# First layer of a fused four-layer kernel: the compression network of the keys loaded early, and compressed attention moved ahead of the local pairs

## The chip, the cores and the metric

The kernel runs on one core of one Trainium2 chip. The metric is device time in microseconds (us) of one execution; where several executions were timed, the median is given. One further execution was taken by the hardware profiler, and the rows below are of that one.

## The reference, cut to what matters

256 tokens of 1024 numbers go through two layers of attention and feed-forward, and then through two mixer blocks. All of it is float32. The change touches the attention of the first layer alone. That layer has eight "A" heads with three gated branches and eight "B" heads with a sliding window and sinks:

```python
def compress_blocks(t, pe, w1, w2):
    chunks = t.reshape(bsz, hkv, seq // CMP_STRIDE, CMP_STRIDE, dh)
    blocks = jnp.concatenate([chunks[:, :, :-1], chunks[:, :, 1:]], axis=-2)
    blocks = (blocks + pe).reshape(bsz, hkv, nc, CMP_BLOCK * dh)
    return jax.nn.silu(blocks @ w1) @ w2          # w1: 2048 x 256
...
# layer 0
z = h @ w_in_e                                    # queries, six key/value groups, gates, B's q, k, v
kc, vc = compress_blocks(akc, pe_k, wk1, wk2), compress_blocks(avc, pe_v, wv1, wv2)
o_cmp = softmax(q_plain . kc) . vc                # 15 compressed tokens
o_sel = softmax(q_rot . selected keys) . values
o_win = softmax(q_rot . window keys) . values
a_out = g0 * o_cmp + g1 * o_sel + g2 * o_win
x = x + concat(a_out, swa_sink_attention(bq, bk, bv, sinks)) @ w_out_e
```

With 256 tokens the selected branch sees every causal block, so both o_sel and o_win are plain causal attention with different keys.

## The kernel before

The tokens lie as two tiles of 128 partitions. A dense product of this kernel is three TensorE passes (`mm3`, lines 249 to 252): activations and weights are each split into a high and a low part of the type fp32r, and high times high, high times low and low times high are added up in one PSUM bank. The weights come from memory in the order of the program: SP issues one DMA after another (`load`, line 175; `raw_block`, line 216) into five buffers of 128x1024 float32 that are named `wr`. A block is split by ScalarE, which writes the high part `wh` (line 236), and by VectorE, which subtracts it and writes the low part `wl` (line 237). `wh` and `wl` have five buffers each. A DMA into a `wr` buffer waits until the last reader of the block before has ended.

The order of the instructions of each engine is fixed when the program is built: a scheduler takes the program as it is written, with its own estimate of durations, and fills each engine's queue. PSUM has two banks for `psd` tiles, four for `psb` and two for `psm`; one attention pair takes two of the four `psb` banks.

The first layer's input projection w_in_e comes in chunks. Chunk 0 (selected keys and values, raw keys for compression, gates) and chunk 1 (the A queries, with and without rotation, `qr` and `qp`) stand first. `chunk2()` makes the window keys and values, the raw values for compression and the B keys. `chunk3()` and `chunk4()` make the B values and the B queries, in four blocks of 128x768 and two of 128x1024; `bq` (line 688) rotates a query tile, transposes it (line 693) and copies it out on ScalarE.

Around these stand the attention steps. `attend` (line 349) does two heads: products of queries and keys (line 358, a stretch of 64 rows for each head, so that two heads can stand side by side in the array), mask and maximum on VectorE (line 366), exponential on ScalarE (line 367), six transposes on TensorE (line 375), a copy of the transposed probabilities on VectorE for one head (line 381) and ScalarE for the other (line 379), and the products with the values (line 358 again). `nsa_pair(br, j)` calls it for branch br (0 selected, 1 window) and heads 2j and 2j+1 and adds into `accA` (lines 398 and 727); `b_pair(j)` does so for the B heads into `accB`.

`compress` (line 636) builds the blocks (line 640 on TensorE, 647 and 649 on VectorE), multiplies them with the 2048 x 256 weights (line 656, 64 products of 32 columns by 256, unsplit float32 straight from `wr`), transposes and sums, and applies SiLU. `keys_cmp` and `values_cmp` use it; each loads its weights as four blocks of 128x1024 into `wr`, and a block stays there until the products of line 656 are done. `attend_cmp` is the attention on the 15 compressed tokens: scores (line 774), a chain of ten VectorE steps with one exponential on ScalarE (lines 781 to 792), transposes (795), a ScalarE copy (797), the products with the compressed values (800) and the addition into `accA` (801). At the end `split_T` (line 265) transposes `accA` and `accB` (line 270), and the output projection w_out_e follows.

Of the kernel before, what the change touches and what calls it, by code (L numbers as in the profile page):

```python
# [18 lines left out]
P = 128  # L19
# [4 lines left out]
BLK = 1024  # L24
# [123 lines left out]
def model(ctx: ExitStack, tc: tile.TileContext, A, out, taps=None):  # L148
    nc = tc.nc
# [66 lines left out]
    def raw_block(src, off, n):  # L216
        raw = tmp([BLK], "wr", "wr")
        load(raw[:, :n], bass.AP(tensor=src.tensor, offset=src.offset + off, ap=[[n, P], [1, n]]))
        return raw
# [332 lines left out]
    def layer0(nm, after):  # L552
# [69 lines left out]
        kz = {0: keys_T(ksd)}  # L622

        w = win.get(1)
        for t in range(2):
            o = psb()
            dense(o, nm.T(t), w)
            r = nm.rstd[t]
            q0 = tmp([512], "w512", "q0")
            nc.scalar.activation(q0, o, AF.Copy, scale=r)  # L630
            q1 = tmp([512], "w512", "q1")
            rope(q1.rearrange("p (h d) -> p h d", h=8), o.rearrange("p (h d) -> p h d", h=8), r, 8, 64, t)
            headsT(qr, q1, t)
            headsT(qp, q0, t)

        def compress(dup, pe_b, w1):
            p = psm()
            for g in range(2):
                for t in range(2):
                    nc.tensor.transpose(p[:, g * 256 + t * P:g * 256 + (t + 1) * P],  # L640
                                        dup[t][:, g].rearrange("p a d -> p (a d)"), ident)
            b = tmp([2, 256], "w512", "blk")
            pg = p.rearrange("p (g t) -> p g t", g=2)
            ij = lambda x: x.rearrange("p g (i j) -> p g i j", j=16)
            for a in range(2):
                s = slice(64 * a, 64 * a + 64)
                nc.vector.tensor_tensor(ij(b[s, :, 0:240]), ij(pg[s, :, 16 * a:16 * a + 240]),
                                        pe_b[s, None, None, :].to_broadcast([64, 2, 15, 16]), op=ALU.add)
            nc.vector.tensor_copy(b[:, :, 240:256], pg[:, :, 240:256])
            bj = b.rearrange("p g (i j) -> p (g i) j", j=16)  # L650
            ph = psm()

            for part in range(4):
                wt = raw_block(w1, part * P * BLK, BLK)
                for j in range(4):
                    nc.tensor.matmul(ph[32 * j:32 * j + 32, :256], bj[:, :, part * 4 + j], wt[:, j * 256:(j + 1) * 256],
                                     start=(part == 0), stop=(part == 3), skip_group_check=True)
            z = tmp([256], "qk", "cz")
            nc.scalar.activation(z, ph[:, :256], AF.Copy)
            p2 = psm()  # L660
            for cb in range(2):
                nc.tensor.transpose(p2[:, cb * P:(cb + 1) * P], z[:, cb * P:(cb + 1) * P], ident)
            e, h, u = (small(64, n_) for n_ in ("ce", "ch", "cu"))
            nc.vector.tensor_reduce(u.rearrange("p (a b) -> p a b", a=2), p2[:, :256].rearrange("p (a c b) -> p a b c", a=2, c=4),
                                    axis=AX.X, op=ALU.add)
            nc.scalar.activation(e, u, AF.Exp, scale=-1.0)
            nc.vector.tensor_scalar(e, e, 1.0, None, op0=ALU.add)
            nc.vector.reciprocal(e, e)
            nc.vector.tensor_tensor(h, u, e, op=ALU.mult)
            return h  # L670
# [25 lines left out]
        def chunk3():  # L696

            w = win.get(3)
            for t in range(2):
                o = psd()  # L700
                dense(o[:, :384], nm.T(t), w)
                nc.scalar.activation(vt[t][:, 2, :, 0:64], hv2(o[:, 0:128]), AF.Copy, scale=nm.rstd[t])
                bq(o[:, 128:384], qb[0], nm.rstd[t], t)
# [38 lines left out]
            weighted(pair_of(accB, j), pov, rc)  # L742

        def keys_cmp():
            hk = compress(kcd, pe[:, 0, :], A["cmp_k_w1"])
            pk = psm()
            for cb in range(2):
                nc.tensor.matmul(pk[:, :32], w2k[:, cb].rearrange("p a d -> p (a d)"), hk[:, cb * 32:(cb + 1) * 32],
                                 start=(cb == 0), stop=(cb == 1))
            for g in range(2):  # L750
                nc.vector.tensor_copy(kcz[g][0:64, 0, 0:15], pk[0:64, g * 16:g * 16 + 15])
                nc.vector.tensor_copy(kcz[g][64:128, 1, 0:15], pk[64:128, g * 16:g * 16 + 15])

        def values_cmp():
            hv = compress(vcd, pe[:, 1, :], A["cmp_v_w1"])
            hvx = tmp([2, 8, 16], "qk", "hvx")
            for cb in range(2):
                for g in range(2):
# [48 lines left out]
            return lambda k: (mixT[t, k // 4][0][:, k % 4, :], mixT[t, k // 4][1][:, k % 4, :])  # L807

        nsa_pair(0, 0)
        nsa_pair(0, 1)  # L810
        chunk2()
        nsa_pair(0, 2)
        keys_cmp()
        nsa_pair(0, 3)
        nsa_pair(1, 0)
        nsa_pair(1, 1)
        nsa_pair(1, 2)
        vbd = values_cmp()
        nsa_pair(1, 3)
        chunk3()  # L820
        chunk4()
        attend_cmp(vbd)
        b_pair(0)
        b_pair(1)
        b_pair(2)
# [529 lines left out]
```

## Time and profile before

| what | value |
|---|---|
| three runs | 1586.75, 1581.74, 1588.69 us; median 1586.75 us |
| profiled execution | 1581.74 us, of which the span (first to last instruction) is 1580.0 us |
| TensorE busy | 1557.5 us, 99% of the span |
| VectorE, ScalarE, GpSimd busy | 982.3, 855.3, 140.3 us |
| data moved by DMA | 269.53 MB, mean 171 GB/s |
| granted TensorE clock | 0.9 or more of full speed in all 40 slices |

The profile gives each engine's busy time, the instructions with their durations, the granted clock, and for each idle stretch what ended it. PE is TensorE, DVE is VectorE, ACT is ScalarE, POOL is GpSimd, and SPq is the queue on which SP issues the weight DMAs. The stretch that the change touches runs from about 20 us, where chunk 1 is being multiplied, to about 127 us, where the output projection of the first layer is being multiplied.

### The profile page before, as it was taken

Reading aid. Unit: us, or ns where it says so; the run is one execution under the profiler, and the core shown is the slowest. Engines: PE = TensorE matmul, PEld = TensorE weight load, DVE = VectorE, ACT = ScalarE, POOL = GpSimd, SP = SyncE. Lnnn points to the kernel's source line nnn. Section 1 sums busy time; section 2 is a strip of 40 time slices with the busy share of each in tenths; the row PEclk is TensorE's granted clock in tenths of the full one; section 3 lists DMA queues with packets and bytes.
Section 4 is the critical chain, followed back from the end, with each engine's and each line's share of the span. In section 5 each row is a group of like instructions: output and inputs, shape, how many; then the busy total and the mean of one; then the engine's idle time right before and its main releaser. Section 6 shows DMA issues by size and latency. Waiting matters only on the chain.

```text
span 1580.0 us, 21686 instructions
## 1 busy us (share of the span) xinstructions
PE 1557.5 (99%) x7870; PEld 1314.7 (83%) x7870; DVE 982.3 (62%) x1778; ACT 855.3 (54%) x1385; POOL 140.3 (9%) x226
## 2 busy tenths in 40 slices
PE   8999999999999999999999999999999999999997
PEld 7778888899888888899888888888898888888886
DVE  6685545577765455576677655456575777655556
ACT  6555444455454444676474654446685564644445
POOL 2000000011100000120033000000020023000001
PEclk9999999999999999999999999999999999999999
DMA  7424655544545565451657555554552656465661
GB/s 270 149 92 133 206 184 184 187 141 131 182 131 191 186 192 188 161 180 40 196 179 233 174 181 192 186 188 160 177 169 71 204 189 197 161 201 185 197 195 61
DMA packets 80587, 269.53 MB, mean 171 GB/s; under 512 B 11360, under 2 KB 12768, under 8 KB 80480
## 3 DMA queue, kind: packets, MB, share of 16 engines
q1 hardware_dynamic: 80048, 267.10, 52.7%
q8 instruction: 62, 1.02, 0.3%
q10 hardware_dynamic: 432, 1.05, 0.2%
q14 instruction: 45, 0.37, 0.1%
HBM read 267.06 MB, written 1.05 MB: 170 GB/s over the span
## 4 chain that ended last, share of the span: by engine, by line
PE 96%; DVE 2%; ACT 1%; DMA 1%; issue 0%; POOL 0%; POOLq 0%; SPq 0%; DVEq 0%; ACTq 0%
PE psb L250 13%; PE psb L252 13%; PE psb L251 13%; PE psd L252 12%; PE psd L250 12%; PE psd L251 12%; PE psb L358 5%; PE psm L250 3%; PE psm L251 3%; PE psm L252 3%; PE psb L375 1%; PE psb L497 1%; DVE wl L237 1%; PE psb L270 1%; PE psm L270 1%; DMA wr<-w_in_e 1%
## 5 line engine op out<-in xcount | busy, mean ns | idle before, releaser
L237 DVE TENSOR_TENSOR wl<-wr,wh 128x1024 fp32r<-128x1024 f32 (+2 forms) x504 | 598.1, 1198 | 423.0 <-ACT wh L236 410.5
L236 ACT ACTIVATE wh<-wr 128x1024 fp32r<-128x1024 f32 (+2 forms) x504 | 512.6, 1029 | 474.0 <-PE psb L252 208.5
L251 PE MATMUL psb<-wl,th 128*128 128x512 f32 x912 | 349.4, 391 | 0.0
L252 PE MATMUL psb<-wh,tl 128*128 128x512 f32 x912 | 349.2, 390 | 0.0
L250 PE MATMUL psb<-wh,th 128*128 128x512 f32 x912 | 346.5, 391 | 0.0
L252 PE MATMUL psd<-wh,tl 128*128 128x512 f32 (+4 forms) x696 | 255.7, 370 | 3.4 <-DVE tl L279 3.4
L250 PE MATMUL psd<-wh,th 128*128 128x512 f32 (+4 forms) x696 | 258.2, 375 | 0.0
L251 PE MATMUL psd<-wl,th 128*128 128x512 f32 (+4 forms) x696 | 255.0, 369 | 0.5 <-DVE wl L237 0.5
L252 PEld LDWEIGHTS psb<-wh,tl 128*128 128x128 f32 x912 | 171.2, 188 | 35.7
L250 PEld LDWEIGHTS psb<-wh,th 128*128 128x128 f32 x912 | 171.3, 188 | 35.3
L251 PEld LDWEIGHTS psb<-wl,th 128*128 128x128 f32 x912 | 171.3, 188 | 35.2
L252 PEld LDWEIGHTS psd<-wh,tl 128*128 128x128 f32 x696 | 131.2, 188 | 22.7 <-DVE tl L279 5.0
L251 PEld LDWEIGHTS psd<-wl,th 128*128 128x128 f32 x696 | 131.5, 189 | 17.5 <-DVE wl L237 0.9
L250 PEld LDWEIGHTS psd<-wh,th 128*128 128x128 f32 x696 | 131.3, 189 | 17.5 <-issue 1.7
L306 POOL TENSOR_SCALAR rest<-ss 128x1 f32<-128x1 f32 x24 | 7.2, 299 | 919.4 <-ACT junk L316 919.4
L367 ACT ACTIVATE pr<-pr,m 128x128 f32<-128x128 f32 (+1 forms) x144 | 58.3, 447 | 29.9 <-DVE m L366 28.1
L250 PE MATMUL psd<-wh,hth 128*128 128x512 f32 x176 | 71.9, 412 | 0.0
L251 PE MATMUL psd<-wl,hth 128*128 128x512 f32 x176 | 68.8, 391 | 0.0
L251 PE MATMUL psm<-wl,hth 128*128 128x512 f32 x176 | 68.5, 389 | 0.0
L250 PE MATMUL psm<-wh,hth 128*128 128x512 f32 x176 | 68.5, 389 | 0.0
L252 PE MATMUL psm<-wh,htl 128*128 128x512 f32 x176 | 67.8, 389 | 0.0
L487 ACT ACTIVATE sg<-psb,r 128x256 f32<-128x256 f32 x88 | 41.8, 475 | 48.0 <-PE psb L252 47.8
(320 smaller groups left out, 1759.9 us busy)
## 6 DMA issues: line engine op xcount, KB each, us to landing
wr<-w_gate_up SPq DMA_DIRECT2D x176, 512.0 KB, 4.3
wr<-w_down SPq DMA_DIRECT2D x88, 512.0 KB, 3.3
wr<-w_in SPq DMA_DIRECT2D x88, 512.0 KB, 4.0
wr<-w_qkv_o SPq DMA_DIRECT2D x32, 384.0 KB, 3.5
wr<-w_o SPq DMA_DIRECT2D x16, 512.0 KB, 4.1
wr<-w_ple_gate SPq DMA_DIRECT2D x16, 512.0 KB, 4.0
wr<-w_in_e SPq DMA_DIRECT2D x10, 512.0 KB, 4.7
wr<-w_out_e SPq DMA_DIRECT2D x8, 512.0 KB, 4.6
```

The source lines that it names most:

```text
L236: nc.scalar.activation(hi[:, :m * n], raw, AF.Copy)
L237: nc.vector.tensor_tensor(lo[:, :m * n], raw, hi[:, :m * n].bitcast(F32), op=ALU.subtract)
L250: first = nc.tensor.matmul(o, xh, wh, start=start, stop=False)
L251: nc.tensor.matmul(o, xh, wl, start=False, stop=False)
L252: nc.tensor.matmul(o, xl, wh, start=False, stop=stop)
L270: turns.append(nc.tensor.transpose(p[:, j * P:(j + 1) * P], src[:, j * P:(j + 1) * P], ident))
L306: nc.gpsimd.tensor_scalar(rest, ms, self.eps, None, op0=ALU.add)
L358: mm = lambda o, l, r, a, b: nc.tensor.matmul(o, l, r, start=a, stop=b, skip_group_check=True)
L367: exps.append(nc.scalar.activation(e, e, AF.Exp, bias=neg, scale=-1.0))
L375: nc.tensor.transpose(bank[j][:, b * P:(b + 1) * P], pr[:, j, b * P:(b + 1) * P], ident)
L487: nc.scalar.activation(sg, o[:, :256], AF.Silu, scale=r)
L497: nc.tensor.transpose(pt[:, j * 256 + t * P:j * 256 + (t + 1) * P], hs[t][:, j * P:(j + 1) * P], ident)
```

## The change

The change loads the keys' compression weights ahead of chunk 2's weights, as eight DMAs of 128x512 into buffers named `xt` (there are 16 of them; the layer's norm uses eight, the transposed mixed heads use eight later) instead of four DMAs of 128x1024 into `wr`. The order of the calls becomes: pair (0,0), `keys_cmp`, pair (0,1), chunk 2, `values_cmp`, pairs (0,2) and (0,3), `attend_cmp`, pairs (1,0), (1,1) and (1,2), chunk 3, pair (1,3), chunk 4, the four B pairs, the output projection. Line numbers behind `chunk1` move by 6 to 10: what was 656 is 662, 693 is 699, 727 is 733, 781 to 792 are 791 to 802, 795 is 805, 797 is 807, 800 is 810 and 801 is 811. The product of `values_cmp` with its second weights, line 764, is line 774 after the change, and the scores of compressed attention, line 774, are line 784.

```diff
@@ -622,6 +622,12 @@
         kz = {0: keys_T(ksd)}
 
         w = win.get(1)
+
+        w1k = []
+        for h in range(8):
+            w1k.append(tmp([512], "xt", "w1"))
+            at = A["cmp_k_w1"].offset + (h // 2) * P * BLK + (h % 2) * 512
+            load(w1k[h], bass.AP(tensor=A["cmp_k_w1"].tensor, offset=at, ap=[[BLK, P], [1, 512]]))
         for t in range(2):
             o = psb()
             dense(o, nm.T(t), w)
@@ -651,9 +657,9 @@
             ph = psm()
 
             for part in range(4):
-                wt = raw_block(w1, part * P * BLK, BLK)
+                wt = w1(part)
                 for j in range(4):
-                    nc.tensor.matmul(ph[32 * j:32 * j + 32, :256], bj[:, :, part * 4 + j], wt[:, j * 256:(j + 1) * 256],
+                    nc.tensor.matmul(ph[32 * j:32 * j + 32, :256], bj[:, :, part * 4 + j], wt[j],
                                      start=(part == 0), stop=(part == 3), skip_group_check=True)
             z = tmp([256], "qk", "cz")
             nc.scalar.activation(z, ph[:, :256], AF.Copy)
@@ -742,7 +748,7 @@
             weighted(pair_of(accB, j), pov, rc)
 
         def keys_cmp():
-            hk = compress(kcd, pe[:, 0, :], A["cmp_k_w1"])
+            hk = compress(kcd, pe[:, 0, :], lambda part: [w1k[2 * part + j // 2][:, j % 2 * 256:j % 2 * 256 + 256] for j in range(4)])
             pk = psm()
             for cb in range(2):
                 nc.tensor.matmul(pk[:, :32], w2k[:, cb].rearrange("p a d -> p (a d)"), hk[:, cb * 32:(cb + 1) * 32],
@@ -752,7 +758,11 @@
                 nc.vector.tensor_copy(kcz[g][64:128, 1, 0:15], pk[64:128, g * 16:g * 16 + 15])
 
         def values_cmp():
-            hv = compress(vcd, pe[:, 1, :], A["cmp_v_w1"])
+            def w1(part):
+                wt = raw_block(A["cmp_v_w1"], part * P * BLK, BLK)
+                return [wt[:, j * 256:(j + 1) * 256] for j in range(4)]
+
+            hv = compress(vcd, pe[:, 1, :], w1)
             hvx = tmp([2, 8, 16], "qk", "hvx")
             for cb in range(2):
                 for g in range(2):
@@ -807,19 +817,19 @@
             return lambda k: (mixT[t, k // 4][0][:, k % 4, :], mixT[t, k // 4][1][:, k % 4, :])
 
         nsa_pair(0, 0)
+        keys_cmp()
         nsa_pair(0, 1)
         chunk2()
+        vbd = values_cmp()
         nsa_pair(0, 2)
-        keys_cmp()
         nsa_pair(0, 3)
+        attend_cmp(vbd)
         nsa_pair(1, 0)
         nsa_pair(1, 1)
         nsa_pair(1, 2)
-        vbd = values_cmp()
+        chunk3()
         nsa_pair(1, 3)
-        chunk3()
         chunk4()
-        attend_cmp(vbd)
         b_pair(0)
         b_pair(1)
         b_pair(2)
```

Three places of the new order matter below. The first is SP's queue, the weight DMAs of the first layer, before (`wr<-w_in_e 128x1024 x8` is chunks 1 and 2, `128x768` chunk 3, the next two chunk 4):

```order
L176 DMA w2v<-cmp_v_w 128x128
L176 DMA wr<-w_in_e 128x1024 x8
L176 DMA wr<-cmp_k_w 128x1024 x4
L176 DMA wr<-cmp_v_w 128x1024 x4
L176 DMA wr<-w_in_e 128x768 x4
L176 DMA wr<-w_in_e 128x1024 x2
L176 DMA wr<-w_out_e 128x1024 x8
```

and after:

```order
L176 DMA w2v<-cmp_v_w 128x128
L176 DMA wr<-w_in_e 128x1024 x4
L176 DMA w_325<-cmp_k_w 128x512
...
L176 DMA w_339<-cmp_k_w 128x512
L176 DMA wr<-w_in_e 128x1024 x4
L176 DMA wr<-cmp_v_w 128x1024 x4
L176 DMA wr<-w_in_e 128x768 x4
L176 DMA wr<-w_in_e 128x1024 x2
L176 DMA wr<-w_out_e 128x1024 x8
```

The keys' weights moved from behind chunk 2 to ahead of it and out of the `wr` buffers; the values' weights stay ahead of chunks 3 and 4 and hold four of the five `wr` buffers until their products are done.

The second place is TensorE's queue at compressed attention. Before, with `hvx` the hidden compressed values, `qp` the unrotated queries, `cs` the scores, `ppT` their transposed probabilities and `vbd` the compressed values:

```order
L774 MATMUL psm<-kcz_194,qp 128x32 x2
L774 MATMUL psm<-kcz_196,qp 128x32 x2
L358 MATMUL psb<-vt,pt 128x65 x6
...
L375 MATMUL psb<-S,pr 128x128 x9
L358 MATMUL psb<-vt,pt 128x65 x6
L375 MATMUL psb<-S,pr 128x128 x3
L358 MATMUL psb<-vt,pt 128x65 x3
L795 MATMUL psm<-S,cs 128x128 x2
...
L800 MATMUL psm<-vbd,ppT 128x512 x2
```

and after:

```order
L358 MATMUL psb<-vt,pt 128x65 x6
L774 MATMUL psm<-w2v,hvx 128x64
L784 MATMUL psm<-kcz_194,qp 128x32 x2
L784 MATMUL psm<-kcz_196,qp 128x32 x2
L784 MATMUL psm<-kcz_194,qp 128x32 x2
L784 MATMUL psm<-kcz_196,qp 128x32 x2
L774 MATMUL psm<-w2v,hvx 128x64
L805 MATMUL psm<-S,cs 128x128 x2
L810 MATMUL psm<-vbd,ppT 128x512 x2
L699 MATMUL psm<-S,q_1030 128x128 x2
L699 MATMUL psm<-S,q_1067 128x128 x2
L358 MATMUL psb<-kz,qr 128x128
```

Before, two B pairs' products stand between the scores and the transposes of the probabilities; after, one product of 64 columns. All dense products of chunks 3 and 4 stand ahead of this piece after the change.

The third place is ScalarE's queue where the splits of the first w_out_e blocks stand. Before (`pr` is the exponential of a pair, `cz` the compression network's first layer):

```order
L236 ACTIVATE wh_1084<-wr_1082 128x1024
L367 ACTIVATE pr_802<-pr_802,m_801 128x256
L666 ACTIVATE ce_920<-cu_922 128x64
L236 ACTIVATE wh_1400<-wr_1398 128x1024
L702 ACTIVATE vt_190<-psd_1002,r_171 128x2x64
L379 ACTIVATE pt_803<-psb_805 128x384
L236 ACTIVATE wh_1406<-wr_1404 128x1024
```

and after:

```order
L236 ACTIVATE wh_1408<-wr_1406 128x1024
L665 ACTIVATE cz_727<-psm_702 128x256
L236 ACTIVATE wh_1414<-wr_1412 128x1024
L236 ACTIVATE wh_1446<-wr_1444 128x1024
L367 ACTIVATE pr_861<-pr_861,m_860 128x128
L367 ACTIVATE pr_861<-pr_861,m_860 128x256
L236 ACTIVATE wh_1452<-wr_1450 128x1024
L367 ACTIVATE pr_861<-pr_861,m_860 128x128
L367 ACTIVATE pr_861<-pr_861,m_860 128x256
L672 ACTIVATE ce_732<-cu_734 128x64
L367 ACTIVATE pr_901<-pr_901,m_900 128x128
```

Four splits of w_out_e now stand directly ahead of the exponentials of pairs (1,0) and (1,1) or between them.

## Rows read from the trace of the kernel before

**Rows 1.** The page's first part: the span, and TensorE's busy time.
```profile
span 1580.0 us, 21686 instructions
...
PE 1557.5 (99%) x7870; PEld 1314.7 (83%) x7870; DVE 982.3 (62%) x1778; ACT 855.3 (54%) x1385; POOL 140.3 (9%) x226
```

**Rows 2.** The page's fourth part: shares of the chain that ended last, by engine.
```profile
PE 96%; DVE 2%; ACT 1%; DMA 1%; issue 0%; POOL 0%; POOLq 0%; SPq 0%; DVEq 0%; ACTq 0%
```

**Rows 3.** Busy time by stretch; per engine (instructions); then clock, DMA share, GB/s.
```profile
43.00:127.00 84.00, 80.10 (x597) 66.08 (x597) 64.28 (x249) 43.66 (x100) 5.71 (x9) 1.00 0.34 114
...
99.00:105.00 6.00, 4.27 (x30) 2.72 (x30) 5.54 (x32) 3.71 (x10) 0.00 (x0) 1.00 0.08 31
...
60.00:80.00 20.00, 20.00 (x154) 17.24 (x154) 15.39 (x51) 11.70 (x24) 0.00 (x0) 1.00 0.74 256
```

**Rows 4.** TensorE from 43 to 127 us by line: busy, mean ns | idle before, releaser.
```profile
L375 PE MATMUL psb<-S,pr 128*128 128x128 f32 x72 | 12.2, 281 | 2.2 <-ACT pr L367 1.9
...
L358 PE MATMUL psb<-kz,qb 64*128 64x128 f32 (+1 forms) x32 | 4.9, 349 | 0.9 <-DVE acc L727 0.9
```

**Rows 5.** SP's queue in order of time: start, us until the last was issued.
```profile
33.37 23.79 SPq L176 DMA_DIRECT2D wr<-cmp_v_w  x4
```

**Rows 6.** The page's sixth part: DMAs, KB each, median us from issue to landing.
```profile
wr<-w_qkv_o SPq DMA_DIRECT2D x32, 384.0 KB, 3.5
...
wr<-w_out_e SPq DMA_DIRECT2D x8, 512.0 KB, 4.6
```

**Rows 7.** The chain of waits from 66 to 78 us: start, us, what.
```profile
66.18 1.94 PE psm L656 x32
...
68.44 8.06 DMA wr<-w_in_e
...
76.59 1.06 ACT wh L236
```

**Rows 8.** The wr tiles, 20 to 95 us: ns min/median/max of the splits.
```profile
L237 DVE TENSOR_TENSOR wl<-wr,wh x17: 948/1215/1357, 19.8 to 91.3; 128x1024 fp32r<-128x1024 f32 x13, 128x768 fp32r<-128x768 f32 x4
...
L236 ACT ACTIVATE wh<-wr x16: 842/1052/1062, 20.6 to 94.0; 128x1024 fp32r<-128x1024 f32 x12, 128x768 fp32r<-128x768 f32 x4
```

**Rows 9.** VectorE in order of time, 88 to 112 us: start, us, what.
```profile
88.36 0.68 DVE L766 TENSOR_TENSOR vbd<-psm,C 128x512 f32<-128x512 f32 x1
...
98.00 0.42 DVE L781 TENSOR_TENSOR cs<-psm,C 128x256 f32<-128x256 f32 x1
...
98.91 0.17 DVE L784 TENSOR_TENSOR cm<-cm,C 128x16 f32<-128x16 f32 x1
...
100.22 0.35 DVE L366 CUSTOM_DVE_ANT_0 pr<-psb,BM,nsinks 128x128 f32<-128x128 f32 x1 [0.40 <-PE psb L358]
...
100.49 0.86 DVE L727 SCALAR_TENSOR_TENSOR acc<-psb,cf,acc 128x64 f32<-128x64 f32 x4
...
104.18 0.24 DVE L790 RECIPROCAL crc<-cd 128x16 f32<-128x16 f32 x1
...
111.10 0.69 DVE L801 TENSOR_TENSOR acc<-acc,psm 128x512 f32<-128x512 f32 x1 [0.27 <-PE psm L800]
```

**Rows 10.** ScalarE in order of time, at 31 us and from 99 to 108 us.
```profile
31.02 1.06 ACT L236 ACTIVATE wh<-wr 128x1024 fp32r<-128x1024 f32 x1 [0.49 <-PE psb L252]
...
99.58 0.42 ACT L787 ACTIVATE cs<-cs 128x256 f32<-128x256 f32 x1 [2.68 <-DVE cs L785]
...
100.67 0.40 ACT L367 ACTIVATE pr<-pr,m 128x128 f32<-128x128 f32 x1 [0.68 <-DVE m L366]
...
107.60 0.38 ACT L797 ACTIVATE ppT<-psm 128x256 f32<-128x256 f32 x1 [0.35 <-PE psm L795]
```

**Rows 11.** TensorE in order of time: two pairs' products of queries and keys.
```profile
99.26 0.93 PE L358 MATMUL psb<-kz,qb 64*128 64x128 f32 x8
...
107.43 0.92 PE L358 MATMUL psb<-kz,qb 64*128 64x128 f32 x4
```

## The prediction

> **What bounds the kernel now.** I read the busy times of the engines first: TensorE works 1557.5 us of a span of 1580.0 us [rows 1], so at most 22.5 us of idle time exist in the whole program, and work taken from another engine is worth nothing by itself. The chain of waits says the same: TensorE is 96% of it, VectorE 2%, ScalarE and DMA 1% each [rows 2]. Then I cut out the stretch that the change touches, 43 to 127 us: TensorE is busy 80.10 of 84.00 us there, so 3.9 us are idle [rows 3]. The reader is to see in those two numbers that little can be won: the change moves work and removes none. Third, I asked which waits make up the 3.9 us. By line, 2.2 us stand ahead of the transposes of the probabilities (1.9 of them ended by the exponentials) and 0.9 us ahead of the B pairs' products, ended by VectorE's additions into the accumulator [rows 4]. Between 99 and 105 us TensorE is busy only 4.27 of 6.00 us [rows 3]; there two B pairs stand with little other work beside them. The weights look worse than they are: SP's queue stands for 23.79 us at the values' weights [rows 5], and a landing of 8.06 us stands in the chain behind the 1.94 us of the values' products [rows 7], but from 60 to 80 us TensorE is busy 20.00 of 20.00 us [rows 3]. That landing is hidden by attention work.
>
> **The change part by part.** Products, splits, exponentials and bytes are the same before and after; only places change.
>
> *Keys' weights early, into other buffers.* Eight DMAs for four, 2.1 MB ahead of chunk 2's weights. At the 256 GB/s of a busy stretch [rows 3] these bytes take 8.2 us, and the next landings behind them come that much later. Cover: the last split of chunk 2 waited for TensorE and not for its load (0.49 us idle, ended by a product of chunk 1 [rows 10]), so its block had landed by then. I take 0; the upper end is one whole landing of a block, 4.6 us [rows 6]. The keys no longer hold `wr` buffers, which can remove the block of SP's queue at 33 us [rows 5], but nothing waited for that, so no gain is booked.
>
> *T1, compressed attention without cover.* In the new order of TensorE one product of 64 columns stands between the scores and the transposes of the probabilities. The chain between them is: addition of the mask 0.42, then `vbd` 0.68 in VectorE's queue, maximum 0.42, 0.17, subtraction 0.42, exponential 0.42 on ScalarE, sum 0.42, 0.17, reciprocal 0.24, 0.17, scaling 0.42. The rows give 0.68, 0.42, 0.17 and 0.24 [rows 9] and the exponential's 0.42 [rows 10]; the four other steps over 256 columns are priced as line 781, the two other small ones as line 784. That is 3.95 us, and with the copy behind the transposes, 0.38 [rows 10], 4.3 us. Before, the first of these steps began at 98.00 [rows 9] and the copy at 107.60 [rows 10], with two B pairs' work on TensorE between them. Bounds: 3.5 (some of pair (0,3)'s products slip into it) and 4.6.
>
> *T2, the accumulator behind it.* The two products with `vbd` need one `psm` bank each, and each addition into `accA`, 0.69, has four smaller additions of a pair, 0.86, between it and the other [rows 9]. 0.69 + 0.86 + 0.69 = 2.24 until the banks are free for the next transposes of queries and scores; then a mask 0.35 [rows 9] and an exponential 0.40 [rows 10] before the next pair's transposes can start. Together 3.0. Bounds 1.5 and 4.
>
> *T3, exponentials behind splits.* On ScalarE four splits of w_out_e stand ahead of or among the exponentials of pairs (1,0) and (1,1). The loads of three of these blocks wait until the values' products have freed their buffers, and then take 4.6 us [rows 6]. 4 × 1.05 [rows 8] = 4.2 us, less the 0.8 us that the masks need anyway, is 3.4. Bounds: 0, if the scheduler's guess of the landings is right, and 5.
>
> *T4, chunk 3 and 4 through one buffer.* Four of the five `wr` buffers hold the values' weights until their products, which now stand behind most of chunk 3 and half of chunk 4. So six blocks go through the fifth, each 3.5 us of landing [rows 6] and two splits of 0.84 and 0.95 [rows 8], 5.3 us. The second block's products stand only some six products behind the first's; later on the keys' products and a pair's transposes fill the gap. Bounds 0 and 5.3; I take a third, 1.9.
>
> *T5, B pairs 2 and 3 bare.* No dense product is left beside them. The nearest rows are those of 99 to 105 us, where 1.73 of 6.00 us are idle [rows 3]; with 0.5 for the second pair's copy, 2.2. Bounds 1 and 3.
>
> *What is won.* All idle time of 43 to 127 us, 3.9 us, is taken as removed, since chunk 3 now fills the early pairs. The products of queries and keys of two heads take 0.93 us side by side, and 0.92 for each head alone [rows 11]. Before, three pairs were apart; after, two: 0.85 won.
>
> Sum: 4.3 + 3.0 + 3.4 + 1.9 + 2.2 = 14.8; less 3.9 and 0.85 is **+10.0 us**. Against the profiled execution (1581.74 us, 1.7 us of it outside the span) that is 1591.8. This execution was also the fastest of the three runs; the median, 1586.75, stands 5.0 above it, so the predicted median is **1596.8 us**. With every term at its lower bound (3.5 + 1.5 + 0 + 0 + 1 − 4.75) the change costs 1.3 us, 1588.0; with every upper bound 4.6 + 4 + 5 + 5.3 + 3 + 4.6 − 4.75 = 21.8 us, 1608.6.
>
> **Rivals.** *1: the waits are not there (not slower).* The scheduler had its own estimate of each duration when it put TensorE's queue into this order; if the values' weights land before they are asked for, and pairs (1,0) and (1,1) find their masks done, T2 to T5 shrink and T1 alone stands against 4.75 us won. At T1 + T2 + T3 + T4 + T5 below 4.75 the change is no loss. For it: chunk 3's products now fill 43 to 60 us, where attention stood alone, and SP's block of 23.79 us [rows 5] goes. Against: T1 is a chain of fixed durations without other work. If T1's 4.3 is all that is left, the time is 1586.3; if even that is covered, 1582.0. It cannot gain much more: 4.75 us is 0.3%.
> The Trainium skill, page "DMA: Bandwidth & Descriptors", section "Rules for kernel authors", speaks for this rival: issue a transfer early, compute, and wait for it late. By that rule the keys' landing leaves the path; the rows of 60 to 80 us show that it was not on TensorE's path before.
>
> *2: the single buffer is the bound (slower still).* T4 counts 3.5 us for a landing, but the landing in the chain took 8.06 us [rows 7] where several transfers were in flight. If the values' four loads and the keys' eight share the engines with chunk 3's, two blocks of chunk 3 are late by 4.6 us more each, of which the pairs beside them cover 2: about 7 us more, 1603.8.
>
> *3: the clock.* The granted clock is 1.00, that is 2.4 GHz, in each of the stretches [rows 3], also where TensorE was busy only 4.27 of 6.00 us. Between compressed attention and the output projection the new order has four pairs' products of queries and keys, 0.93 us each [rows 11], and their 24 transposes, 0.28 each [rows 4]: 10.4 us of work between waits of a size that no stretch of before shows. If the clock fell to its lower level, 1.2 GHz, for half of it, 5.2 us would take 10.4: 1602.0.
> The Trainium skill, page "TensorE: Matmul & The Clock Gate", section "HAM oscillation — how this bites in real kernels", says that idle gaps between bursts of matmuls make the clock fall back. The trace agrees only in that it shows no such gap and no fall.
>
> *4: chunk 2 is late.* The early keys' loads cost their upper end, 4.6 us, and the rest is as forecast: 1601.4.
>
> **How the numbers follow.** A change of under 0.5%, 7.9 us, is about what a measurement of this kernel cannot tell from none. Forecast: 0.58. Its own range is 1591 to 1602, and about two thirds of it lie over 1594.7, where slower by 0.5% begins: 0.39 slower, 0.19 same. Rival 1: 0.22, of which 0.19 same and 0.03 faster (the work elsewhere in the program would have to gain as well). Rival 2: 0.12, slower. Rival 3: 0.04, slower. Rival 4: 0.04, slower. Sum: faster 0.03, same 0.38, slower 0.59. The range goes from 1585.5, which takes in most of rival 1, to 1605.0, above rival 2's time.
>
> **What would show it.** Right: on TensorE an idle gap of 3 to 4 us between the scores (line 784) and the transposes of line 805, ended by VectorE's line 802, a smaller one behind line 810 ended by line 811, and one ahead of the transposes of pairs (1,0) or (1,1) ended by ScalarE's exponentials, with splits of w_out_e just ahead of them. T4 shows as idle ahead of products of chunk 3, ended by line 237. TensorE's idle time from 43 us until the output projection, 3.9 before, should be about 14.8. Wrong: if the transposes of line 805 follow without a gap, or that idle time is under 8 us, the sum is wrong; a lower granted clock in that stretch makes it rival 3; chunk 2's first product later than its place would allow makes it rival 4.

## The result, and the profile after

The change makes the kernel slower: median 1596.33 us (7 executions, 1592.39 to 1598.83) against 1586.75 us (7 executions, 1581.74 to 1588.69). The ratio is 1.0065, with a 95% interval of 1.0046 to 1.0084 (it is not the quotient of the two medians, which would be 1.0060). The profiled execution took 1596.93 us, 15.2 us over the profiled one of before.

First the page of the changed kernel: its span, the busy times, the granted clock in 40 slices, and the shares of the chain that ended last.

```profile
span 1595.1 us, 21694 instructions
...
PE 1567.4 (98%) x7870; PEld 1320.7 (83%) x7870; DVE 984.4 (62%) x1778; ACT 853.7 (54%) x1385; POOL 140.0 (9%) x226
...
PEclk9979999999999999999999999999999999999999
...
PE 93%; DVE 3%; DMA 2%; ACT 1%; issue 1%; POOL 0%; POOLq 0%; ACTq 0%; DVEq 0%
```

Against [rows 1] TensorE has the same 7870 products and is *busy* 9.9 us longer; its share of the chain fell from 96% [rows 2] to 93%. Waits alone would lengthen the span and leave the busy time as it was. The third slice of the clock, about 80 to 120 us, shows 7.

The same work, from 43 us until the first transposes of x behind the output projection are done, ends at 141.2 us before and at 156.1 us after. The window of before (columns as in [rows 3]):

```profile
43.00:141.20 98.20, 94.30 (x663) 77.83 (x663) 73.31 (x261) 50.60 (x110) 5.71 (x9) 1.00 0.38 127
```

and of after, first the whole, then its three parts, then pieces of 2 us around the two changes of the clock:

```profile
43.00:156.10 113.10, 103.99 (x664) 83.63 (x664) 75.19 (x267) 49.41 (x111) 6.86 (x12) 0.89 0.28 93
...
43.00:85.90 42.90, 40.63 (x329) 33.65 (x328) 33.40 (x119) 24.21 (x55) 4.00 (x8) 1.00 0.44 150
85.90:109.10 23.20, 18.23 (x73) 13.74 (x74) 13.10 (x49) 3.31 (x10) 2.85 (x4) 0.50 0.15 47
109.10:156.10 47.00, 45.13 (x268) 36.24 (x267) 28.69 (x100) 21.89 (x49) 0.00 (x0) 0.99 0.20 64
...
84.00:86.00 2.00, 0.83 (x5) 0.60 (x6) 2.00 (x8) 2.00 (x5) 0.00 (x0) 0.97 0.85 268
86.00:88.00 2.00, 2.00 (x12) 2.00 (x12) 2.00 (x4) 0.35 (x1) 0.00 (x0) 0.50 0.82 250
...
108.00:110.00 2.00, 2.00 (x11) 1.10 (x11) 1.10 (x8) 1.71 (x5) 0.10 (x1) 0.56 0.00 0
110.00:112.00 2.00, 1.97 (x15) 1.56 (x16) 1.81 (x10) 1.63 (x6) 0.00 (x0) 1.00 0.00 0
```

The stretch is 14.9 us longer. Idle time went from 98.20 − 94.30 = 3.90 to 113.10 − 103.99 = 9.11 us, +5.2. Busy time went up by 9.7 us. From 85.90 to 109.10 us the granted clock was 0.50, that is 1.2 GHz, and the mean of 0.56 from 108 to 110 us puts the rise at about 109.8 us. What the clock costs is an estimate: rows of the same work at both clocks, told below, shrink to 0.58 (2.66 and 1.55 us) and to 0.52 (3.78 and 1.98 us) of their time, so the 18.23 us of work would take 7.6 to 8.7 us less at 2.4 GHz. That is most of the 9.7 us.

The gaps and the same work at either clock, on TensorE in order of time:

```profile
75.65 1.55 PE L358 MATMUL psb<-vt,pt 128*128 128x65 f32 x12
...
83.45 0.55 PE L375 MATMUL psb<-S,pr 128*128 128x128 f32 x3 [0.75 <-ACT pr L367]
84.39 0.55 PE L375 MATMUL psb<-S,pr 128*128 128x128 f32 x3 [0.39 <-ACT pr L367]
85.71 2.69 PE L358 MATMUL psb<-vt,pt 128*128 128x65 f32 x12 [0.78 <-ACT pt L379]
...
88.84 2.66 PE L358 MATMUL psb<-vt,pt 128*128 128x65 f32 x12
...
99.70 0.66 PE L805 MATMUL psm<-S,cs 128*128 128x128 f32 x2 [3.94 <-DVE cs L802]
100.89 3.78 PE L810 MATMUL psm<-vbd,ppT 128*128 128x512 f32 x4 [0.53 <-ACT ppT L807]
...
105.60 0.69 PE L699 MATMUL psm<-S,q 128*128 128x128 f32 x2 [0.50 <-POOL q L420]
...
115.61 0.89 PE L358 MATMUL psb<-kz,qb 64*128 64x128 f32 x4 [0.46 <-DVE acc L733]
...
134.69 1.93 PE L375 MATMUL psb<-S,pr 128*128 128x128 f32 x9 [0.23 <-ACT pr L367]
...
141.31 0.44 PE L270 MATMUL psb<-S,acc 128*128 128x128 f32 x2 [0.62 <-DVE acc L398]
```

Twelve products with the values take 1.55 us at 75.65 and 2.66 us at 88.84. The clock fell at about 85.9 us, behind idle gaps of 0.75, 0.39 and 0.78 us within about 3 us, ahead of the large gap of 3.94 us. The reader is to see that the small gaps cost 1.9 us by themselves and came just ahead of a fall that cost more. What stood behind them, on ScalarE in order of time:

```profile
79.67 1.06 ACT L236 ACTIVATE wh<-wr 128x1024 fp32r<-128x1024 f32 x1 [0.27 <-DMA wr<-w_out_e]
80.96 0.80 ACT L367 ACTIVATE pr<-pr,m 128x128 f32<-128x128 f32 x2 [0.23 <-DVE m L366]
81.67 1.04 ACT L236 ACTIVATE wh<-wr 128x1024 fp32r<-128x1024 f32 x1
...
84.24 1.04 ACT L236 ACTIVATE wh<-wr 128x1024 fp32r<-128x1024 f32 x1
```

Splits of w_out_e (1.06, 1.04, 1.04 us) alternate with the exponentials of pairs (1,0) and (1,1), as the order said.

One thing about before has to be told for the rest. Its executions fall into two groups by the granted clock: of 85 beside the experiments, 48 have a mean clock of 0.997 or more (median 1581.8 us, at most 1584.4) and 37 of 0.991 to 0.996 (median 1588.1 us); one more, 2543.48 us at a clock of 0.573, is left out. The profiled execution, 1581.74 at 0.998, is of the first group; the median of the runs that the prediction saw, 1586.75, lies among the times of the second. The seven executions of after all have 0.994 or less, and their time goes with it, from 1592.39 us at 0.994 to 1598.83 us at 0.990.

### The profile page after: what moved, and what is told of

Its sections match the earlier page's. It is cut to its first block, busy times and chain, and to the rows that moved or that the text cites. A ratio compares the mean times of both kernels' runs of the same rounds, so it can differ in the third digit from the quotient of the medians.

```text
span 1595.1 us, 21694 instructions
## 1 busy us (share of the span) xinstructions
PE 1567.4 (98%) x7870; PEld 1320.7 (83%) x7870; DVE 984.4 (62%) x1778; ACT 853.7 (54%) x1385; POOL 140.0 (9%) x226
## 3 DMA queue, kind: packets, MB, share of 16 engines
q10 hardware_dynamic: 432, 1.05, 0.2%
HBM read 267.06 MB, written 1.05 MB: 168 GB/s over the span
## 4 chain that ended last, share of the span: by engine, by line
PE 93%; DVE 3%; DMA 2%; ACT 1%; issue 1%; POOL 0%; POOLq 0%; ACTq 0%; DVEq 0%
PE psb L250 13%; PE psb L252 13%; PE psb L251 13%; PE psd L252 11%; PE psd L250 11%; PE psd L251 11%; PE psb L358 5%; PE psm L250 3%; PE psm L251 3%; PE psm L252 3%; DMA wr<-w_in_e 1%; DVE wl L237 1%; PE psb L497 1%; PE psb L375 1%; PE psb L270 1%; PE psm L270 1%
## 5 line engine op out<-in xcount | busy, mean ns | idle before, releaser
L252 PE MATMUL psd<-wh,htl 128*128 128x512 f32 x176 | 67.5, 391 | 0.0
```

The lines of the kernel that those rows point to most:

```text
L252: nc.tensor.matmul(o, xl, wh, start=False, stop=stop)
```

## The experiments

Three theories went in. Theory C: idle gaps let TensorE's clock fall, and half of the loss is work at 1.2 GHz. Theory W: the loss is the waits by themselves. Theory L: the early load of the keys' weights makes it. Medians are told beside those of before on the same chip, and ratios with their 95% interval. `queue_after(x, list)` puts an instruction behind others in the order without a semaphore.

**The load alone** (the early load of after, the calls in the order of before):

```diff
         nsa_pair(0, 0)
-        keys_cmp()
         nsa_pair(0, 1)
         chunk2()
-        vbd = values_cmp()
         nsa_pair(0, 2)
+        keys_cmp()
         nsa_pair(0, 3)
-        attend_cmp(vbd)
...
-        chunk3()
+        vbd = values_cmp()
         nsa_pair(1, 3)
+        chunk3()
         chunk4()
+        attend_cmp(vbd)
```

> Only the early load of the keys' weights into the xt buffers; the order of the calls is that of before. Theory C (the fall of the granted clock, set off by idle gaps between 82 and 86 us and drawn out by the bare compressed attention, makes up about 9 us of the profiled loss of 15, and TensorE's added idle time 4.6): the load is not involved, so 1583 to 1590 us, within 0.3% of before, and the granted clock stays 1.00 from 43 to 130 us. Theory L (the early load and the buffers it leaves to others cost something by themselves, by a late chunk 2 or by the scheduler's other order): over 1591 us.

Measured: 1590.42 us (11) against 1583.06, ratio 1.0043 (1.0026 to 1.006). TensorE, then the windows:

```profile
54.78 0.76 PE L250 MATMUL psd<-wh,th 128*128 128x384 f32 x2 [1.92 <-ACT wh L236]
```

```profile
54.00:56.00 2.00, 1.22 (x5) 1.22 (x6) 1.04 (x2) 1.48 (x3) 0.00 (x0) 0.77 0.00 0
56.00:58.00 2.00, 2.00 (x8) 2.00 (x7) 0.00 (x0) 0.00 (x0) 0.00 (x0) 0.50 0.53 154
```

Neither theory's forecast holds: theory C had the clock at 1.00, theory L a time over 1591 us. I had not expected the load to cost anything. The scheduler filled the queues in another order once the load was early; chunk 3's products met a split that was late by 1.92 us, and the clock was 0.50 behind that gap, and again from about 92.6 us.

**The order alone** (the new order of the calls, the keys' weights in `wr` as before):

```diff
-            w1k.append(tmp([512], "xt", "w1"))
...
+                wt = raw_block(A["cmp_k_w1"], part * P * BLK, BLK)
+                return [wt[:, j * 256:(j + 1) * 256] for j in range(4)]
```

> The new order of calls with the keys' weights loaded as before, four blocks into wr at the place where keys_cmp is called. Theory C: the order makes the bare compressed attention, whatever the load; a gap of 3 to 4 us ahead of the transposes of the compressed probabilities and a half-clock stretch: 1590 to 1598 us. Theory L (the early load alone costs 7 us, as measured, and so makes most of the loss of the change): within 3 us of before, 1583 to 1586 us.

Measured: 1596.67 us (6) against 1586.74, ratio 1.0072 (1.005 to 1.0095). The order without the early load makes the whole loss, so theory L falls: the load is not needed for it, though alone it costs 0.4%. The two do not add up. The gap of the compressed softmax is there, 4.47 us:

```profile
95.41 0.66 PE L803 MATMUL psm<-S,cs 128*128 128x128 f32 x2 [4.47 <-DVE cs L800]
```

The clock fell inside that gap, at 94.7 us, was back at 101.5 us, and was at 0.50 once more from 111.7 to 118.6 us.

**Work in the gap** (five products that nobody reads, between the compressed scores and the transposes):

```diff
+            fillers = [queue_after(nc.tensor.matmul(pT[:, 256:512], ident, C[:, :256], start=True, stop=True, skip_group_check=True), [score]) for _ in range(5)]
-                nc.tensor.transpose(pT[:, t * P:(t + 1) * P], pp[:, t * P:(t + 1) * P], ident)
+                queue_after(nc.tensor.transpose(pT[:, t * P:(t + 1) * P], pp[:, t * P:(t + 1) * P], ident), fillers)
```

> The changed kernel with five products of 256 columns more, between the scores and the transposes of compressed attention; their result is read by nobody. Theory C: the added work keeps TensorE busy in the gap of 3.9 us, so the half clock, which the gaps before it set off, ends earlier; 1590 to 1595 us, below the changed kernel although it does more. Theory W (the idle waits are the loss, the clock is a bystander): the products fit into the gap, 1595 to 1599 us, and the clock rows are as in the changed kernel.

Measured: 1594.38 us (11) against 1583.06, ratio 1.0063 (1.0045 to 1.0082). TensorE, then the windows:

```profile
101.38 1.98 PE L811 MATMUL psm<-vbd,ppT 128*128 128x512 f32 x4 [0.53 <-ACT ppT L808]
...
104.86 0.41 PE L699 MATMUL psm<-S,q 128*128 128x128 f32 x2 [1.08 <-DVE acc L812]
```

```profile
86.00:88.00 2.00, 1.73 (x10) 1.73 (x11) 2.00 (x4) 0.91 (x3) 0.00 (x0) 0.68 0.83 244
...
100.00:102.00 2.00, 1.47 (x6) 0.80 (x6) 0.81 (x3) 0.38 (x1) 0.00 (x0) 0.91 0.00 0
```

The fall stays, at 86.7 us, and so do small gaps ahead of it (0.97, 0.29 and 0.77 us). But with TensorE at work where it idled 3.94 us, the clock is back at about 100.4 us instead of 109.8, and the products with `vbd` that took 3.78 us take 1.98. In time this run does not differ from the change beyond the intervals. Idle time that is filled with work nobody needs is no time won, so the median alone does not tell C from W here; the clock's rows do. Nine executions at 0.991 to 0.994 took 1592.5 to 1598.5 us, two at 0.997 took 1588.82 and 1589.28.

**Splits behind the exponentials** (w_out_e's splits behind the exponentials of pairs (1,0) and (1,1)):

```diff
-            nc.scalar.activation(hi[:, :m * n], raw, AF.Copy)
+            queue_after(nc.scalar.activation(hi[:, :m * n], raw, AF.Copy), getattr(self, "behind", []))
...
+        wo.w.behind = exps[16:24]
```

> The changed kernel with the splits of w_out_e on ScalarE put behind the exponentials of pairs (1,0) and (1,1). Theory C: the three gaps ahead of the transposes and products of these pairs (0.75, 0.39 and 0.78 us) go, TensorE's clock stays at 1.00 at least until compressed attention, and its half-clock stretch of 23 us goes or is under 10 us: 1585 to 1591 us, mean granted clock 0.996 or more. Theory W: 1.9 us of idle time and perhaps 2 of the gap in compressed attention are saved, the half clock stays: 1592 to 1594.5 us.

Measured: 1590.49 us (11; 1588.88 to 1591.25) against 1583.06, ratio 1.0037 (1.0024 to 1.005). TensorE, then the windows:

```profile
95.86 0.66 PE L805 MATMUL psm<-S,cs 128*128 128x128 f32 x2 [5.03 <-DVE cs L802]
```

```profile
92.00:94.00 2.00, 0.00 (x0) 0.00 (x0) 1.71 (x7) 0.33 (x1) 0.00 (x0) 0.84 0.86 309
94.00:96.00 2.00, 0.14 (x1) 0.17 (x2) 1.74 (x6) 0.09 (x1) 0.00 (x0) 0.50 0.77 264
...
100.00:102.00 2.00, 1.23 (x5) 0.49 (x4) 1.85 (x7) 0.40 (x2) 1.28 (x2) 0.95 0.00 0
```

The small gaps of 83 to 86 us are gone, and with them the fall at 85.9. The clock falls at 93.4 now, inside the large gap, and is back at 100.2: 6.8 us at half speed instead of 23.9. The time lies in theory C's range and not in W's.

**Both together** (the edits of the last two):

> The changed kernel with both edits: splits of w_out_e behind the exponentials of pairs (1,0) and (1,1), and five unread products of 256 columns in compressed attention. With the splits late alone the trace shows one gap of 5.03 us and one of 1.17, and a half-clock stretch from 93.4 to 100.1 us. Theory C (gaps let the clock fall, and the fall makes most of the loss): with the gap filled by 2.5 us of products the clock stays up in most executions, 1585 to 1589 us, mean granted clock 0.997 or more. Theory W (idle time alone counts): as with the splits late alone, 1589.5 to 1592 us.

Measured: 1590.78 us (12) against 1586.74, ratio 1.0037 (1.0021 to 1.0054). TensorE, then VectorE:

```profile
93.41 0.41 PE L806 MATMUL psm<-S,cs 128*128 128x128 f32 x2 [4.27 <-DVE cs L802]
```

```profile
88.22 2.34 DVE L237 TENSOR_TENSOR wl<-wr,wh 128x1024 fp32r<-128x1024 f32 x2
```

A miss of theory C's time; 1590.78 lies in W's range. The five products ran from 85.48 to 87.9, ahead of the gap, and did not fill it: as with the late splits alone, the splits' subtractions stand among the softmax's steps on VectorE, and the gap is 4.27 us where it was 5.03. The clock was low for 3.4 us only, from 93.9 to 97.3, and six of the 12 executions have 0.997. They still took 1588.6 to 1591.5 us: most of what is left of the loss there is waits.

**Compressed attention back behind chunk 4** (T1 undone, the rest of the change kept):

```diff
         nsa_pair(0, 3)
-        attend_cmp(vbd)
         nsa_pair(1, 0)
...
         chunk4()
+        attend_cmp(vbd)
```

> The changed kernel with attend_cmp back behind chunk 4, where it stood before, so that pair (1,2) and the B pairs cover its chain on VectorE. Theory C: the gaps at 82 to 86 us are still there, so the clock still falls at about 86 us, but without the gap of 3.9 us it rises again sooner: 1589 to 1593 us, half clock for 5 to 15 us. Theory W: 4.5 us less than the changed kernel, 1590 to 1593 us, with the half-clock stretch as long as before. The clock rows tell the two apart, the time hardly.

Measured: 1592.73 us (9) against 1583.06, ratio 1.0046 (1.0028 to 1.0064). Three executions at clock 0.996 took 1588.2 to 1589.2, six at 0.991 took 1592.3 to 1593.6. TensorE of the profiled one (at 0.996), then the windows:

```profile
83.58 0.55 PE L375 MATMUL psb<-S,pr 128*128 128x128 f32 x3 [0.87 <-ACT pr L367]
84.51 0.55 PE L375 MATMUL psb<-S,pr 128*128 128x128 f32 x3 [0.39 <-ACT pr L367]
85.83 1.55 PE L358 MATMUL psb<-vt,pt 128*128 128x65 f32 x12 [0.78 <-ACT pt L379]
...
93.50 0.55 PE L375 MATMUL psb<-S,pr 128*128 128x128 f32 x3 [1.34 <-ACT pr L367]
```

```profile
92.00:94.00 2.00, 0.66 (x5) 0.31 (x3) 2.00 (x13) 1.74 (x5) 0.67 (x1) 1.00 0.00 0
94.00:96.00 2.00, 1.94 (x15) 1.89 (x15) 0.95 (x4) 0.64 (x2) 0.06 (x1) 0.80 0.00 0
```

The bare softmax is not needed for a fall. Here gaps of 0.87, 0.39 and 0.78 us at 83 to 86 us, nearly those of after, were followed by none in the profiled execution (the twelve products behind them take 1.55 us), which both theories had wrong; behind one of 1.34 us at 93.5 the clock was low from about 95.2 to 105.4. So the same gaps do not always end in a fall.

**Four more ways to cover the gaps, and one kernel of before.** In the order of their edits: chunk 4's last products put behind the compressed scores as cover, with the splits behind the exponentials;

```diff
+            first = mm3(o, xh, xl, wh, wl, i == 0, i == len(w) - 1)
+            if i == 3:
+                queue_after(first, behind)
...
+                dense(o[:, :256], nm.T(t), w, scored if t else ())
...
+        wo.w.behind = exps[16:24]
```

> The changed kernel with the splits late and real work as cover: the last 15 products of chunk 4's second tile are put behind the scores of compressed attention, so nothing is added. Theory C: no gap over 2.5 us is left, the clock stays up in most executions: 1583 to 1587 us, mean granted clock 0.997 or more. Theory W: 1.9 us of the 5.03 us gap are covered, the gap moves in part to the exponentials: 1588 to 1590.5 us.

the splits still later, behind the exponentials of pair (1,3), `wo.w.behind = exps[28:32]` and no cover;

> The changed kernel with the splits of w_out_e put behind the exponentials of pair (1,3), so that neither ScalarE's exponentials of (1,0) and (1,1) nor VectorE's chain of compressed attention has a split in it. In the earlier edit the five subtractions of w_out_e, 1.22 us each, had only moved into that chain. The chain alone is then 4.0 us, covered by 12 products with the values and 6 transposes. Theory C (gaps, and the fall of the clock behind them): one gap of 2.5 us or less, the clock at 1.00 in most executions, 1583 to 1587 us at a mean clock of 0.997 or more. Theory W: the idle time falls by 4 us against the first edit, but the time in step with it only: 1586 to 1588 us with clocks as mixed as before.

both of these, with the cover at `i == 2`;

> As the run beside it (splits behind the exponentials of pair (1,3)), and 18 products of chunk 4's second tile behind the scores of compressed attention as cover. Theory C: the gap ahead of the compressed probabilities' transposes is 1.5 us or less, no gap elsewhere over 0.8; the clock stays at 1.00 in nearly all executions: 1581 to 1585 us, mean clock 0.998. Theory W: 1584 to 1587 us. If the bare exponentials of pairs (1,0) and (1,1) now make a gap of 1.5 us or more instead, the gain is nil: 1587 us.

and the splits one at a time, so that no two stand together:

```diff
+            queue_after(nc.scalar.activation(hi[:, :m * n], raw, AF.Copy), self.behind.pop(0) if getattr(self, "behind", []) else [])
...
+            ppTs.append(nc.scalar.activation(ppT, pT[:, :256], AF.Copy))
...
+        wo.w.behind = [[], exps[16:24], ppTs, exps[24:28], exps[28:32]]
```

> The changed kernel with the five w_out_e splits that had stood in a row put one at a time: the first where it was, the second behind the exponentials of pairs (1,0) and (1,1), the third behind compressed attention's last ScalarE copy, the fourth and fifth behind the exponentials of pairs (1,2) and (1,3). Theory C (the clock falls behind a gap of 2 us and more, wherever the gap is put; five splits in a row were such a gap in each edit so far): no gap over 1.5 us is left, idle time from 43 us to the output projection 4 to 6 us, the clock at 1.00 in most executions, 1582 to 1587 us at a mean clock of 0.997. Theory W: the same idle time, but clocks of 0.994 as in the edits before, 1588 to 1592 us.

Measured, in this order: 1592.51 (12) against 1586.74, ratio 1.0037 (1.0021 to 1.0054); 1594.56 (6) against 1582.32, 1.0066 (1.0046 to 1.0085); 1593.95 (6) against 1582.32, 1.0063 (1.0045 to 1.0082); 1588.38 (12) against 1582.93, 1.0023 (1.0007 to 1.0038). The largest gap of each on TensorE, in the same order:

```profile
92.78 0.66 PE L809 MATMUL psm<-S,cs 128*128 128x128 f32 x2 [4.94 <-DVE cs L806]
```

```profile
102.92 2.82 PE L358 MATMUL psb<-vt,pt 128*128 128x65 f32 x12 [3.12 <-ACT pt L379]
```

```profile
105.16 2.17 PE L360 MATMUL psb<-vt,pt 128*128 128x65 f32 x12 [3.73 <-ACT pt L381]
```

```profile
90.45 0.66 PE L807 MATMUL psm<-S,cs 128*128 128x128 f32 x2 [1.91 <-DVE cs L804]
```

The windows at the fall, first of the splits still later and of the splits one at a time:

```profile
100.00:102.00 2.00, 0.00 (x0) 0.00 (x0) 2.00 (x3) 2.00 (x3) 0.00 (x0) 0.86 0.48 145
102.00:104.00 2.00, 1.08 (x5) 1.08 (x6) 2.00 (x3) 1.24 (x3) 0.00 (x0) 0.50 0.88 291
```

```profile
90.00:92.00 2.00, 1.02 (x3) 0.65 (x4) 1.22 (x4) 0.79 (x2) 0.00 (x0) 0.57 0.00 0
```

The first three took longer than either theory's range, because the gap went elsewhere instead of away; the last, 1588.38 us, lies in W's range, just above C's. Five blocks of w_out_e are split close together in the new order, each 1.05 us on ScalarE and 1.2 us on VectorE. Put behind the exponentials, they stand in the softmax chain (4.94 us); put later still, that gap is 0.22 us (0.91 with the cover), but they stand ahead of a copy of probabilities (3.12 and 3.73 us). With the later splits the clock fell where the gap had been put, at about 101 us (the windows above) and 106 us. Only one at a time do they do less harm: the largest gap is 1.91 us, the idle gaps that the profile names sum to about 4.3 us, and this is the best version of the new order: 1.0023 against the change's 1.0065. The clock still fell at its gap, though that is under 2 us, and it does not beat before.

The last edit is to *before*: work where its two B pairs stood bare at 99 to 105 us [rows 3]. Eight unread products stand behind the products of queries and keys of B pairs 0 and 1, and the second half of `attend_cmp` behind B pair 0.

```diff
+        for i in range(2 * spare):
+            queue_after(mm(bank[i % 2][:, 384:512], ident, ident, True, True), [last])
...
-        attend_cmp(vbd)
+        rest = attend_cmp(vbd)
         b_pair(0)
+        rest()
```

> The kernel before with eight unread products of 128 columns behind the queries' and keys' products of B pairs 0 and 1, in the stretch where TensorE is idle 1.73 of 6 us, and the second half of compressed attention tied behind the first B pair. Its own executions lie in two groups, 1581 us at a clock of 0.998 and 1587.5 at 0.994. Theory C: with that stretch filled the group at 0.994 goes: all executions at 0.997 or more and 1580.5 to 1583.5 us, although TensorE does about 1 us more. If the group at 0.994 stays, the clock falls somewhere else in it, or without a gap.

Measured: 1583.0 us (12; 1581.86 to 1586.36) against 1582.32, ratio 1.0 (0.9987 to 1.0013). The stretch's window:

```profile
99.00:105.00 6.00, 5.35 (x44) 4.03 (x43) 5.82 (x32) 3.18 (x9) 0.00 (x0) 1.00 0.07 27
```

TensorE is busy 5.35 of 6.00 us there instead of 4.27. All 12 executions have a clock of 0.997 or more, where before has 5 of 17 at 0.991 to 0.994 on the same chip and 37 of 85 in all. The slower group was not seen. Eight executions took 1581.9 to 1583.0 us, as the faster group does, but four at 0.997 took 1584.9 to 1586.4 us, longer than any of that group and than theory C's range; these four were not explained.

A second profile of the kernel before was taken to catch its slower group:

> The kernel before once more, for a trace. Its 29 timed executions lie in two groups, about 1581 us at a mean granted clock of 0.998 and about 1587.5 us at 0.991 to 0.994. Theory C: this trace either shows the clock at 1.00 from 20 us on and about 1581 us, or a half-clock stretch around the bare B pairs at 99 to 105 us and about 1587 us, with the idle waits the same in both. Theory W: both groups differ in idle time, not in the clock.

It took 1580.83 us at clock 0.998 and shows no fall in this stretch, so where the clock falls in that group was never seen.

## Why the prediction was right, and where only its number was

The time is right, 1596.8 against 1596.33, and the sign. The mechanism is half right, and that the number came out so close is luck, two errors that cancel: the forecast for a profiled execution was 1591.8, and it took 1596.93, since the sum left out the 9.7 us of longer busy time and had 5.7 us of idle time too much (14.8 for 9.11); the 5.0 us that were then added as "the median stands 5.0 above it" are, by their size, the distance of before's two groups, read as scatter. After's median stands 0.6 us below its profiled execution.

- **The keys' weights early, 0.** As costed: no wait for chunk 2's weights shows. That it would cost nothing in any order was not said and is not so (1.0043 alone).
- **T1, 4.3.** The gap and the one behind the copy are 3.94 + 0.53 = 4.47 us, at line 805, ended by line 802, as named.
- **T2, 3.0.** 0.50 + 0.46 = 0.96 us, and neither is ended by line 811, as the prediction had it: GpSimd's step of the query rotation (line 420) ends the first, a pair's addition (line 733) the second. The additions take what was said, but while the clock is low the four products ahead last 3.78 us and hide the wait. With work in the gap, where they take 1.98 us, the wait shows: 1.08 us ended by that addition (line 812 there).
- **T3, 3.4.** 0.75 + 0.39 + 0.78 = 1.92 us, at the place named. The exponentials end the first two; ScalarE's copy of the transposed probabilities (line 379), behind the split of 84.24, ends the third.
- **T4, 1.9.** (A third of 5.3 would be 1.8.) Idle time of 0.27 us from 43 to 60 us, where most of chunk 3's products stand; up to 85.90 us all idle time is 2.27 us, and 1.92 of that is T3. The window of 43 to 60 us of after:

```profile
43.00:60.00 17.00, 16.73 (x134) 13.92 (x134) 12.35 (x44) 9.02 (x23) 4.00 (x8) 1.00 0.24 70
```

  SP's queue does wait for the single buffer, as its rows in order of time show (they answer to [rows 5]), for 27.77 us with the six blocks of chunks 3 and 4, but attention covers it:

```profile
24.56 11.68 SPq L176 DMA_DIRECT2D wr<-cmp_v_w  x4
38.49 27.77 SPq L176 DMA_DIRECT2D wr<-w_in_e  x6
```

- **T5, 2.2.** 0.23 + 0.62 = 0.85 us. The five terms come to 8.47 of the 9.11 us idle, against 14.8 forecast.
- **Won, 3.9 and 0.85.** The waits of before are gone as assumed. The saving from two pairs side by side does not show: with the 7.6 to 8.7 us of the clock taken off, the busy time would be 95.3 to 96.4 us against 94.30.

So idle time grew by 5.2 us and not by 10.9 (14.8 less 3.9), and **rival 3, the clock, given 0.04, makes an estimated 7.6 to 8.7 us**. The step that failed is the sentence that weighed it: the granted clock of before is 1.00 "also where TensorE was busy only 4.27 of 6.00 us". That was one execution of a kernel that in 37 of 85 runs has a lower clock, and the three times shown, 1581.74 apart from 1586.75 and 1588.69, already said that something of 5 to 7 us comes and goes. The rival was also put at the wrong place, behind the softmax chain, and at 5.2 us; the fall began 10 us ahead of that chain's gap, behind T3's gaps. Rivals 1, 2 and 4 did not happen.

The Trainium skill, page "TensorE: Matmul & The Clock Gate", section "HAM oscillation — how this bites in real kernels", says that idle gaps between bursts of matmuls make the clock fall back. The runs agree in that: in after and in four experiments that moved the gap (splits behind the exponentials, compressed attention back, splits still later, splits one at a time) the fall moved along (at about 85.9, 93.4, 95.2, 101.4 and 90.3 us).

Theory W alone does not stand, and neither does the clock alone: after at one clock is estimated at 1588.2 to 1589.3 us, 6.5 to 7.6 over the profiled execution of before, and that is mostly the waits' part. Runs bear this out: the 15 executions of the experiments on the new order that have a clock of 0.997 took 1586.0 to 1591.5 us, all above the 1584.4 us that before's faster group reaches at most. What stays open is why the same gaps are followed by a fall in one execution and not in another (compressed attention back behind chunk 4), and where before's second group loses its 6.3 us; the run with work at 99 to 105 us suggests that stretch and does not show it.

## What to carry to other kernels

Where TensorE is nearly always busy, a reordering that opens idle gaps costs the gaps and then, in many executions, the work behind them at half clock: look for rows of busy time that grew with the same number of instructions. Look at the clock of every execution before a median is set beside one profiled execution; a distance between them may be a mechanism and not scatter. Work that is only moved off one chain (here five splits in a row) lands on the next one, so spread it out.

## What was not expected of the hardware

The kernel before, unchanged, has two times, 1581.8 and 1588.1 us, that go with mean granted clocks of 0.997 or more and 0.991 to 0.996. Three gaps of under 0.9 us each stood ahead of a fall in after and of none in the profiled execution with compressed attention back, and a stretch at half clock lasted from 3.4 us with both edits together to 23.9 us in after.
